# One width for every expert's first tokens, a hinted branch for the rest, and a smaller block for experts of 65 to 128 tokens

## The chip, the cores and the metric

The kernel runs on one core of a Trainium2 chip. The metric is device time in microseconds (us) for one execution. Five engines work side by side and meet through semaphores: TensorE (PE, with its weight loads shown as PEld), VectorE (DVE), ScalarE (ACT), GpSimd (POOL) and SyncE (SP), which here issues most of the transfers. Each engine has its own instruction stream and takes its own branches.

## The reference

One decoder layer on 512 tokens of width 1024: two kinds of token mixing, cross attention, and a mixture of 32 experts, of which every token uses two. Only the last part is touched:

```
g_prob = softmax(xt @ w_group + b_group); best group       # 4 groups of 8 experts
top 2 of softmax(expert logits inside the group)           # 2 experts per token
per expert e: hid = silu(xblk @ w_gate[e]) * (xblk @ w_up[e])
              y   = hid @ w_down[e]                        # 1024 -> 512 -> 1024
out = sum of y * weight over each token's two experts
```

All of it is float32. The 1024 assignments fall unevenly on the experts. With these inputs experts 0 to 31 get 41, 41, 19, 5, 15, 74, 64, 9, 0, 4, 14, 1, 21, 11, 55, 28, 10, 92, 53, 14, 14, 133, 30, 162, 2, 19, 34, 6, 17, 11, 4 and 21 tokens. So 22 experts have at most 32, six have 33 to 64 and four have more than 64: experts 5 (74), 17 (92), 21 (133) and 23 (162). These counts are known only when the program runs.

## The kernel before

The kernel works through the layer in stages; routing ends some 590 us into the profiled execution, and the experts follow. The weights of an expert are 6 MB in six transfers of 1 MB (gate g0, g1, up u0, u1, down d0, d1). SP issues them in expert order (`pump`, the transfer is L815) into a ring of 20 places. A transfer can start when the place's former weights, 20 transfers earlier, have been read for the last time, and it says so by a semaphore of PE.

The loop over experts (L1251 to L1275) is written out 32 times, and the order of instructions on PE, DVE, ACT and POOL is the order in which it is written. For expert `e`:

- `number(e)` (L1211) loads `n` into a register of every engine. Before the loop, `n` was made by counting how many of five limits the expert's number of tokens exceeds (L1044 to L1050): 32, 64, 192, 320 and 448.
- `fetch(rows, later_x[e])` (L1114, on POOL) gathers the tokens behind the first 64 into the one tile `rows` ("xo").
- For odd `e`, `turn_pair` transposes the first 64 tokens of the next two experts on PE (L1122, eight transposes "psgt<-ident,xr").
- A branch on `n > 0` (L1260) chooses `step(now, last, 64)` or `step(now, last, 32)`. A step multiplies the expert's tokens with gate and up (`gate_up`, "psgu"), and in between turns and multiplies down the expert before it (`turn`, "psht<-ident,hs"; `down`, "psy<-wd,hT"). With 64 slots it is 16 matmuls of 512 columns for gate and up, two of them side by side in the array; with 32 slots it is 32 matmuls of 256 columns, four side by side.
- `later_blocks` branches on `n > 1` (L1198). Inside, `block128` computes up to 128 further tokens (transposes "psgt<-ident,xo", then "psg", "psu", "psht<-ident,oh", "psy<-wd,oT"), all in one chain with the result scattered at the end, and a loop (L1202) does further blocks. The loop is not entered with these inputs. An expert's gate and up places in the ring are given back after this branch, since the block may read them.

So every expert's code on PE has two branches of which one or both are jumps: over the width not used, and over the later blocks. The functions that the change touches, and what calls them:

Of the kernel before, what the change touches and what calls it, by code (L numbers as in the profile page):

```python
# [24 lines left out]
KD = D // P  # L25
# [10 lines left out]
FITS = "an expert has at most 512 tokens"  # L36
# [928 lines left out]
def moe(ctx, tc, A, out, x2, x2d, env):  # L965
    nc = tc.nc
    V, SC, PO, PE, SP = nc.vector, nc.scalar, nc.gpsimd, nc.tensor, nc.sync
    bank, ident, before, onesb, f = (env[k] for k in ("bank", "ident", "before", "onesb", "f"))
    tok, mm, pump, W, route, epsr = (env[k] for k in ("tok", "mm", "pump", "W", "route", "epsr"))
# [7 lines left out]
    later_x, later_y = (mc.tile([P, 4, NE], I32, name=f"later_{n}") for n in "xy")  # L977
    ms = ctx.enter_context(tc.tile_pool(name="ms", bufs=1, reuse_waits="tile"))
# [19 lines left out]
    oh, asg = route.oh, route.asg  # L998
# [3 lines left out]
    for i in range(NT):  # L1002
        o = psr[:, i * 32:(i + 1) * 32]
# [8 lines left out]
    d = gp.tile([P, J], F32, name="d")  # L1012
# [29 lines left out]


    steps = iota("steps", [5], [[P, 5]], 0, base=-64)  # L1044
    V.tensor_scalar(steps, steps, 32.0, None, op0=OP.max)
    nb = gp.tile([1, NE, 5], F32, name="nb")
    V.tensor_tensor(nb, cnt[0:1].unsqueeze(2).to_broadcast([1, NE, 5]), steps[0:1].unsqueeze(1).to_broadcast([1, NE, 5]), OP.is_gt)
    nbs = gp.tile([1, NE], F32, name="nbs")
# [48 lines left out]
    def bank(name, tag):  # L1097
        return banks.tile([P, 512], F32, name=name, tag=tag)
# [17 lines left out]

    def turned(xT, rows, copies, tags):

        for a in range(2):
# [2 lines left out]
                PE.transpose(ps[:, k * P:(k + 1) * P], rows[:, a * 512 + k:(a + 1) * 512:4], ident)  # L1122
            copies[a](xT[:, 4 * a:4 * a + 4, :], ps.rearrange("p (k t) -> p k t", t=P))

    class Expert:


        def __init__(self, e):
            self.e, self.c, self.r = e, e // 2, slice(e % 2 * 64, e % 2 * 64 + 64)
            self.x = xT[self.c]  # L1130
            if e % 2 == 0:
                Ys[self.c] = ms.tile([P, D], F32, name="Y", bufs=2)

        def gate_up(self, M, steps):

            e = self.e
            if steps[0] == 0:
                self.ps = bank("psgu", f"g{e % 2}")
            n = P // M // 2
            w = 512 // n  # L1140
            for k in steps:
                for q in range(2 * n):
                    mm(self.ps[q * M:q * M + M, 0:w], self.x[:, k, self.r.start:self.r.start + M],
                       W[e, "ug"[q // n], k // 4][:, k % 4, q % n * w:(q % n + 1) * w], k == 0, k == KD - 1)
            if steps[-1] == KD - 1:
                for q in range(n):
                    h = self.hs[0:M, q * w:(q + 1) * w]
                    SC.activation(h, self.ps[64 + q * M:64 + q * M + M, 0:w], AF.Silu)  # L1148
                    V.tensor_tensor(h, h, self.ps[q * M:q * M + M, 0:w], OP.mult)  # L1149

        def turn(self):
            pt = bank("psht", "h")
            for c in range(4):
                PE.transpose(pt[:, c * 64:(c + 1) * 64], self.hs[:, c // 2 * 256 + c % 2:(c // 2 + 1) * 256:2], ident[0:64, 0:64])  # L1154
            V.tensor_copy(self.hT, pt[:, 0:256])  # L1155

        def down(self):
            e = self.e
            ps = bank("psy", f"y{e % 2}")
            for c in range(4):  # L1160
                for q in range(2):
                    mm(ps[q * 64:q * 64 + 64, :], self.hT[:, c * 64:(c + 1) * 64],
                       W[e, "d", c // 2][:, c % 2, q * 512:q * 512 + 512], c == 0, c == 3)
            for q in range(2):
                SC.copy(Ys[self.c][self.r, q * 512:q * 512 + 512], ps[q * 64:q * 64 + 64, :])  # L1165

        def send(self):
            if self.e % 2:
                scatter(Ys[self.c], first_y[:, self.c:self.c + 1])

    def block128(e, rows, tiles, idx):

        xe, hs, hT = tiles
        tags = "o", f"y{e % 2}"
        turned(xe, rows, (V.tensor_copy, SC.copy), tags)
        ps = {}
        for kind, tag in zip("gu", tags):
            ps[kind] = bank(f"ps{kind}", tag)
            for k in range(KD):
                mm(ps[kind], xe[:, k, :], W[e, kind, k // 4][:, k % 4, :], k == 0, k == KD - 1)  # L1180
            if kind == "g":
                SC.activation(hs, ps["g"], AF.Silu)
        V.tensor_tensor(hs, hs, ps["u"], OP.mult)
# [12 lines left out]
    def later_blocks(e, n, rows):  # L1196

        with tc.If(n > 1):  # L1198
            tiles = [ms.tile([P] + c, F32, name=t) for t, c in (("ox", [KD, P]), ("oh", [512]), ("oT", [512]))]
            block128(e, rows, tiles, later_y[:, 0, e:e + 1])  # L1200
            with tc.If(n > 2):
                with tc.For_i(2, n) as c:  # L1202
                    c = nc.s_assert_within(c - 1, 1, 3, skip_runtime_bounds_check_because=FITS)
                    idx = ms.tile([P, 2], I32, name="oi")
                    for m, t in enumerate((later_x, later_y)):
                        V.tensor_copy(idx[:, m:m + 1], t[:, bass.ds(c, 1), e:e + 1].rearrange("p c e -> p (c e)"))
                    fetch(rows, idx[:, 0:1])
                    block128(e, rows, tiles, idx[:, 1:2])

    def number(e):  # L1210
        return nc.values_load(regs[0:1, e:e + 1], min_val=0, max_val=5, skip_runtime_bounds_check_because=FITS)  # L1211
# [13 lines left out]
    def step(now, last, M):  # L1225

        if M == 64:
            now.gate_up(M, (0, 1))
            last and last.turn()
            now.gate_up(M, (2, 3))  # L1230
            last and last.down()
            now.gate_up(M, (4, 5, 6, 7))
        else:
            now.gate_up(M, (0, 1, 2, 3))
            last and last.turn()
            now.gate_up(M, (4, 5, 6, 7))
            last and last.down()

    with tc.manual_schedule(engines={mybir.EngineType.PE, mybir.EngineType.DVE, mybir.EngineType.Activation, mybir.EngineType.Pool}):
        hs = ms.tile([64, 512], F32, name="hs")  # L1240
        hT = ms.tile([P, 256], F32, name="hT")
        rows = ms.tile([P, D], F32, name="xo")
        fetch_pair(0)
        fetch_pair(1)
        for t in (hs, rows):
            PO.memset(t, 0.0)
        Expert.hs, Expert.hT = hs, hT
        turn_pair(0)
        marks = mark_later_slots()
        last = None  # L1250
        for e in range(NE):  # L1251
            now = Expert(e)
            n = number(e)
            if e > 0:
                fetch(rows, later_x[:, 0, e:e + 1])
            if e % 2 and e < NE - 1:
                turn_pair(e // 2 + 1)
                if e < NE - 3:
                    fetch_pair(e // 2 + 2)
            with tc.If(n > 0) as many:  # L1260
                step(now, last, 64)
            with many.Else():
                step(now, last, 32)
            if last:
                last.send()
                pump(2)
            else:
                later_slots(marks)
                fetch(rows, later_x[:, 0, 0:1])
                cG.close()  # L1270
                env["cT"].close()
# [90 lines left out]
```

## Time and profile before

| | us |
|---|---|
| median of 3 runs (lowest to highest) | 1177.45 (1168.74 to 1178.84) |
| profiled execution, its own time | 1178.46 |
| its span, first to last instruction | 1176.7 |
| PE busy | 991.0 (84%) |
| DVE, ACT, POOL busy | 404.1, 312.6, 279.7 |
| first expert's step to the end of the last one's matmuls | about 590 to 1137 |

In the profile's rows, PE is busy when any matmul runs; a number in square brackets behind a row of the timeline is the time that the engine stood idle ahead of it, with what ended that idle time. "issue" there means that nothing in the profile explains the wait. DMA share is the share of the core's 16 DMA engines that is busy.

### The profile page before, as it was taken

How to read it: one execution, taken by the hardware profiler on the slowest of the kernel's cores; microseconds unless marked ns; L12 is line 12 of the kernel's file. 1: busy time of each engine (PE TensorE's matmuls, PEld its weight loads, DVE VectorE, ACT ScalarE, POOL GpSimd, SP SyncE). 2: the span in 40 equal slices, each digit the busy share in tenths (PEclk: the TensorE clock that was granted, in tenths of full speed). 3: DMA queues.
4: the chain of work that ended last, by engine and by line, in shares of the span. 5: the costliest groups of instructions: out<-in, count | busy, mean ns of one | idle time of the engine just before them, and what ended most of it. 6: DMA issues, size and time to landing. Idle time of an engine off the chain costs nothing. (4 is left out here: it accounts for less than half of the span.)

```text
span 1176.7 us, 16302 instructions
## 1 busy us (share of the span) xinstructions
PE 991.0 (84%) x6260; PEld 649.1 (55%) x6260; DVE 404.1 (34%) x865; ACT 312.6 (27%) x612; POOL 279.7 (24%) x210
## 2 busy tenths in 40 slices
PE   7999999989899999999477997777897887877860
PEld 6787798768688998889223433332332333433320
DVE  8528607656835514345611101111100111011117
ACT  4434423433633534421011101111110101011132
POOL 4431243115124672331211101121101101011112
PEclk9999999999999999999688998898998899998885
DMA  6730231011043452178669959999999949299934
GB/s 206 218 105 24 56 101 37 1 36 55 20 143 93 141 163 71 54 264 332 265 263 413 413 210 397 414 411 414 413 417 400 403 183 407 98 412 412 411 109 180
DMA packets 88618, 269.59 MB, mean 229 GB/s; under 512 B 16191, under 2 KB 57212, under 8 KB 63870
## 3 DMA queue, kind: packets, MB, share of 16 engines
q1 hardware_dynamic: 76926, 252.67, 56.0%
q0 software_dynamic: 10512, 11.04, 2.8%
q10 hardware_dynamic: 1008, 3.67, 0.8%
q8 instruction: 98, 1.61, 0.6%
q14 instruction: 74, 0.61, 0.1%
HBM read 279.91 MB, written 14.68 MB: 250 GB/s over the span
## 5 line engine op out<-in xcount | busy, mean ns | idle before, releaser
L75 PE MATMUL psgu<-wu,xT 128*32 128x256 f32 (+1 forms) x864 | 190.9, 504 | 56.1 <-issue 32.2
L148 POOL TENSOR_TENSOR hl<-raw,hl 128x1024 fp32r<-128x1024 f32 (+1 forms) x67 | 161.4, 2411 | 252.9 <-ACT hl L145 201.9
L75 PE MATMUL psgu<-wg,xT 128*32 128x256 f32 (+1 forms) x864 | 192.8, 504 | 8.7 <-issue 8.7
L75 PEld LDWEIGHTS psgu<-wu,xT 128*32 128x32 f32 (+1 forms) x864 | 66.3, 134 | 151.5 <-issue 119.9
L75 PE MATMUL psy<-wd,hT 128*64 128x512 f32 x512 | 118.4, 600 | 0.7 <-ACTq L1198 0.6
L145 ACT CAST hl<-raw 128x1024 fp32r<-128x1024 f32 (+1 forms) x68 | 70.3, 1040 | 92.0 <-PE psm L75 39.0
L1114 POOL DMA_INDIRECT xo<-x2d,later_x x32 | 32.1, 1004 | 202.8 <-ACTq L1198 55.6
L1155 DVE COPY hT<-psht 128x256 f32<-128x256 f32 x32 | 13.6, 424 | 191.0 <-PE psht L1154 186.2
L1148 ACT ACTIVATE hs<-psgu 32x256 f32<-32x256 f32 (+1 forms) x54 | 22.6, 418 | 208.8 <-PE psgu L75 196.9
L75 PEld LDWEIGHTS psy<-wd,hT 128*64 128x64 f32 x512 | 35.3, 138 | 72.0 <-issue 70.2
L1149 DVE TENSOR_TENSOR hs<-hs,psgu 32x256 f32<-32x256 f32 (+1 forms) x54 | 24.8, 460 | 145.0 <-ACT hs L1148 82.5
L1165 ACT COPY Y<-psy 64x512 f32<-64x512 f32 x64 | 37.1, 580 | 135.2 <-PE psy L75 132.4
L75 PEld LDWEIGHTS psgu<-wg,xT 128*32 128x32 f32 (+1 forms) x864 | 66.8, 134 | 8.7 <-issue 8.4
L75 PE MATMUL psm<-hl,XO 128*128 128x256 f32 x384 | 50.7, 287 | 1.4 <-DVE x L680 1.4
L1122 PE MATMUL psgt<-ident,xr 128*128 128x128 f32 x128 | 22.6, 323 | 33.5 <-PEq L1198 21.2
L75 PE MATMUL psm<-hl,mix 128*128 128x256 f32 x320 | 49.1, 291 | 0.6 <-DVE x L680 0.5
L1106 POOL DMA_INDIRECT yd<-Y,first_y x16 | 16.1, 1009 | 139.4 <-ACTq L1198 125.8
L75 PEld LDWEIGHTS psm<-hl,XO 128*128 128x128 f32 x384 | 47.3, 191 | 2.1 <-DVE x L680 1.8
L75 PE MATMUL psxq<-x1T,hl 128*128 128x512 f32 x192 | 46.7, 396 | 0.0
L75 PEld LDWEIGHTS psm<-hl,mix 128*128 128x128 f32 x320 | 43.5, 193 | 3.5 <-issue 1.3
L75 PE MATMUL psq<-xT,hl 128*128 128x512 f32 x192 | 45.2, 395 | 0.0
L1122 PEld LDWEIGHTS psgt<-ident,xr 128*128 128x128 f32 x128 | 18.5, 212 | 46.2 <-issue 28.9
(368 smaller groups left out, 1669.4 us busy)
## 6 DMA issues: line engine op xcount, KB each, us to landing
wg<-in_moe_w_gate_dram SPq DMA_DIRECT2D x64, 1024.0 KB
wu<-in_moe_w_up_dram SPq DMA_DIRECT2D x64, 1024.0 KB
wd<-in_moe_w_down_dram SPq DMA_DIRECT2D x64, 1024.0 KB
raw<-in_w_in_dram SPq DMA_DIRECT2D x22, 512.0 KB
raw<-in_w_out_dram SPq DMA_DIRECT2D x8, 512.0 KB
raw<-in_xa_wv_dram SPq DMA_DIRECT2D x8, 512.0 KB
raw<-in_xa_wk_dram SPq DMA_DIRECT2D x8, 512.0 KB
raw<-in_xa_wq_dram SPq DMA_DIRECT2D x8, 512.0 KB
```

The source lines that it names most:

```text
L75: PE.matmul(o, l, r, start=start, stop=stop, skip_group_check=True)
L145: cp = SC.copy(hl[:, 0], raw)
L148: (V if n - look < on_dve else PO).tensor_tensor(hl[:, 1], raw, f(hl[:, 0]), OP.subtract)
L1106: t = PO.indirect_dma_start(out=yd, out_offset=bass.IndirectOffsetOnAxis(ap=idx, axis=0), in_=Y, in_offset=None, bounds_check=2 * S - 1, o ...
L1114: PO.indirect_dma_start(out=rows, out_offset=None, in_=x2d, in_offset=bass.IndirectOffsetOnAxis(ap=idx, axis=0), bounds_check=S - 1, oob_i ...
L1122: PE.transpose(ps[:, k * P:(k + 1) * P], rows[:, a * 512 + k:(a + 1) * 512:4], ident)
L1148: SC.activation(h, self.ps[64 + q * M:64 + q * M + M, 0:w], AF.Silu)
L1149: V.tensor_tensor(h, h, self.ps[q * M:q * M + M, 0:w], OP.mult)
L1155: V.tensor_copy(self.hT, pt[:, 0:256])
L1165: SC.copy(Ys[self.c][self.r, q * 512:q * 512 + 512], ps[q * 64:q * 64 + 64, :])
```

## The change

Four things change, all in the experts' part.

1. `step` has one form, with 64 slots, and no branch around it. The first of the five limits becomes 128 in place of 32, so `n` now counts the limits 128, 64, 192, 320 and 448 that are exceeded.
2. `later_blocks` is one branch on `n > 0` with a label. Inside it, `n > 1` (more than 128 tokens) runs `block128` and the loop as before, and otherwise the new `block64` runs.
3. `block64` computes one block of up to 64 tokens with the functions that `Expert` uses for the first 64.
4. In front of each step, PE alone gets a hint that the branch `later{e}` is likely to be taken, that is, that the later code is skipped.

```diff
-    V.tensor_scalar(steps, steps, 32.0, None, op0=OP.max)
+    V.memset(steps[:, 0:1], 128.0)
...
+    def block64(e, rows, tiles, idx):
+
+        xe, hs, hT = tiles[0][:, :, 0:64], tiles[1][0:64], tiles[2][:, 0:256]
+        tags = "o", f"y{e % 2}"
+        for a in range(2):
+            ps = bank("psgt", tags[a])
+            for k in range(4):
+                PE.transpose(ps[:, k * 64:(k + 1) * 64], rows[0:64, a * 512 + k:(a + 1) * 512:4], ident[0:64, 0:64])
+            (SC.copy if a else V.tensor_copy)(xe[:, 4 * a:4 * a + 4, :], ps[:, 0:256].rearrange("p (k t) -> p k t", t=64))
+        ps = bank("psg", "o")
+        gate_up(ps, xe, e, range(KD))
+        hidden(ps, hs)
+        turn(hs, hT)
+        down(bank("psy", tags[1]), hT, e, rows[0:64])
+        scatter(rows, idx)
...
-        with tc.If(n > 1):
-            tiles = [ms.tile([P] + c, F32, name=t) for t, c in (("ox", [KD, P]), ("oh", [512]), ("oT", [512]))]
-            block128(e, rows, tiles, later_y[:, 0, e:e + 1])
-            with tc.If(n > 2):
...
+        with tc.If(n > 0, label=f"later{e}"):
+            with tc.If(n > 1) as more:
+                ts = tiles()
+                block128(e, rows, ts, later_y[:, 0, e:e + 1])
+                with tc.If(n > 2):
...
+            with more.Else():
+                block64(e, rows, tiles(), later_y[:, 0, e:e + 1])
...
-            with tc.If(n > 0) as many:
-                step(now, last, 64)
-            with many.Else():
-                step(now, last, 32)
+            tc.mark_branch_hint_location(f"later{e}", "LikelyTaken", engines=[mybir.EngineType.PE])
+            step(now, last)
```

The functions `gate_up`, `hidden`, `turn` and `down` that `block64` calls are the bodies of the methods of `Expert`, taken out of the class: 16 matmuls of 512 columns, Silu on ACT with a product on DVE, four transposes with a copy, and eight matmuls with two copies on ACT.

On PE, at the end of expert 2's step, where its later code begins. "xo" holds the gathered later tokens, "ox", "oh" and "oT" are the block's tiles. Before:

```order
L1260 UNCONDITIONAL_BRANCH
L1198 COMPARE_AND_BRANCH
L1122 MATMUL psgt<-ident,xo 128x128 x8
L75 MATMUL psg<-wg,ox 128x512 x8
L75 MATMUL psu<-wu,ox 128x512 x8
L1186 MATMUL psht<-ident,oh 128x128 x4
L75 MATMUL psy<-wd,oT 128x512 x8
L1201 COMPARE_AND_BRANCH
```

After the change:

```order
L1221 COMPARE_AND_BRANCH
L1222 COMPARE_AND_BRANCH
L1122 MATMUL psgt<-ident,xo 128x128 x8
L75 MATMUL psg<-wg,ox 128x512 x8
L75 MATMUL psu<-wu,ox 128x512 x8
L1206 MATMUL psht<-ident,oh 128x128 x4
L75 MATMUL psy<-wd,oT 128x512 x8
L1225 COMPARE_AND_BRANCH
```

The jump out of the two widths (L1260) is gone, and the branch to skip (L1221) is followed by the one between the two block sizes (L1222). The block of 128 itself stands as it stood; 36 matmuls lie in it, and 36 more in the loop behind it.

On PE, from the end of expert 2's later code to the first matmul of expert 3, where a skip lands. Before:

```order
L1202 UNCONDITIONAL_BRANCH
L1201 UNCONDITIONAL_BRANCH
L1198 UNCONDITIONAL_BRANCH
L1211 TENSOR_LOAD regs
L1122 MATMUL psgt<-ident,xr 128x128 x8
L1260 COMPARE_AND_BRANCH
L75 MATMUL psgu<-wu,xT 64x512
```

After the change:

```order
L1138 MATMUL psht<-ident,oh 128x64 x4
L75 MATMUL psy<-wd,oT 64x512 x8
L1222 UNCONDITIONAL_BRANCH
L1221 UNCONDITIONAL_BRANCH
L1368 BRANCH_PREFETCH_HINT
L1237 TENSOR_LOAD regs
L1122 MATMUL psgt<-ident,xr 128x128 x8
L75 MATMUL psgu<-wu,xT 64x512
```

The end of the new block of 64 (36 matmuls) now stands last in the skipped code; behind it the hint comes before the register's load, and the step's matmuls follow with no branch between.

## Rows read from the trace of the kernel before

**Rows 1.** The page: span, GB/s in forty slices, the instruction queue.

```profile
span 1176.7 us, 16302 instructions
...
GB/s 206 218 105 24 56 101 37 1 36 55 20 143 93 141 163 71 54 264 332 265 263 413 413 210 397 414 411 414 413 417 400 403 183 407 98 412 412 411 109 180
...
q8 instruction: 98, 1.61, 0.6%
```

**Rows 2.** Stretches: us, engines' busy us (instructions), PE clock, DMA share, GB/s.

```profile
749.00:860.00 111.00, 85.77 (x650) 35.96 (x645) 11.76 (x25) 18.33 (x36) 16.05 (x16) 0.91 1.02 413
...
681.00:695.00 14.00, 11.37 (x27) 4.61 (x25) 2.07 (x3) 0.59 (x1) 0.00 (x0) 0.88 0.04 16
955.00:970.00 15.00, 12.49 (x31) 5.22 (x29) 2.07 (x3) 0.59 (x1) 0.00 (x0) 1.00 0.02 7
1005.00:1025.00 20.00, 18.32 (x45) 7.88 (x43) 1.38 (x2) 1.18 (x2) 0.00 (x0) 1.00 0.01 2
```

**Rows 3.** Waits of SP: us in total, times, longest us.

```profile
SPq L815 <- PEq L1201: 94.7, 4, 33.3
```

**Rows 4.** Timeline of PE, expert 17: step, block of 128, next step.

```profile
848.25 0.64 PE L75 MATMUL psgu<-wu,xT 128*64 128x512 f32 x1
...
859.47 1.23 PE L1122 MATMUL psgt<-ident,xo 128*128 128x128 f32 x8
861.55 7.13 PE L75 MATMUL psg<-wg,ox 128*128 128x512 f32 x16 [0.85 <-DVE ox L1123]
...
877.98 7.10 PE L75 MATMUL psy<-wd,oT 128*128 128x512 f32 x16 [0.83 <-issue]
886.06 0.64 PE L75 MATMUL psgu<-wu,xT 128*64 128x512 f32 x1 [0.98 <-PEq L1201]
```

**Rows 5.** Groups by form, 598 to 1135 us: Silu, product and copy of 64 slots.

```profile
L1148 ACT ACTIVATE hs<-psgu 64x512 f32<-64x512 f32 x9 | 5.3, 594 | 19.4 <-PE psgu L75 19.4
L1149 DVE TENSOR_TENSOR hs<-hs,psgu 64x512 f32<-64x512 f32 x9 | 6.1, 679 | 80.0 <-ACTq L1198 44.4 <-ACT hs L1148 26.7 <-issue 8.9
L1155 DVE COPY hT<-psht 128x256 f32<-128x256 f32 x32 | 13.6, 424 | 191.0 <-PE psht L1154 186.2 <-PE psgu L75 4.8
```

**Rows 6.** Timeline of PE: expert 2's start, and the end of expert 5's block.

```profile
615.26 0.64 PE L75 MATMUL psgu<-wu,xT 128*32 128x256 f32 x2 [5.08 <-PEq L1198]
...
685.24 8.80 PE L75 MATMUL psy<-wd,oT 128*128 128x512 f32 x16 [0.83 <-issue]
```

**Rows 7.** Timeline of PE: ends of blocks 21 and 23, and of expert 31's step.

```profile
962.07 7.11 PE L75 MATMUL psy<-wd,oT 128*128 128x512 f32 x16 [0.83 <-issue]
...
998.34 1.95 PE L1122 MATMUL psgt<-ident,xo 128*128 128x128 f32 x8 [7.06 <-DMA xo<-x2d,later_x]
...
1018.02 7.10 PE L75 MATMUL psy<-wd,oT 128*128 128x512 f32 x16 [0.83 <-issue]
...
1132.70 0.66 PE L1154 MATMUL psht<-ident,hs 64*128 64x64 f32 x4 [0.31 <-PEq L1198]
```

**Rows 8.** Timeline of POOL: the gathers for experts 22 and 23.

```profile
980.63 1.01 POOL L1114 DMA_INDIRECT xo<-x2d,later_x  x1 [8.94 <-DVE xT L1123]
...
989.43 1.01 POOL L1114 DMA_INDIRECT xo<-x2d,later_x  x1 [6.48 <-ACT Y L1165]
```

**Rows 9.** Timeline of PE: first work after expert 24, a 32-slot expert.

```profile
1035.00 1.20 PE L1122 MATMUL psgt<-ident,xr 128*128 128x128 f32 x8 [0.56 <-PEq L1198]
```

**Rows 10.** Timeline of PE: first work after experts 6, 14, 18 and 26, all with 64 slots.

```profile
709.43 1.95 PE L1122 MATMUL psgt<-ident,xr 128*128 128x128 f32 x8 [3.15 <-PEq L1198]
...
817.19 1.20 PE L1122 MATMUL psgt<-ident,xr 128*128 128x128 f32 x8 [2.05 <-DMA xr<-x2d,first_x]
...
899.82 1.42 PE L1122 MATMUL psgt<-ident,xr 128*128 128x128 f32 x8 [2.47 <-PEq L1198]
...
1067.81 1.95 PE L1122 MATMUL psgt<-ident,xr 128*128 128x128 f32 x8 [4.39 <-PEq L1198]
```

**Rows 11.** Timeline of PE: a wait inside a step (expert 3).

```profile
632.44 0.38 PE L75 MATMUL psgu<-wg,xT 128*32 128x256 f32 x1 [2.65 <-issue]
```

More of the change, by code (lines that the diff above doesn't have):

```diff
@@ L1123, in turned, with gate_up, hidden, turn @@
             copies[a](xT[:, 4 * a:4 * a + 4, :], ps.rearrange("p (k t) -> p k t", t=P))
+    def gate_up(ps, x, e, steps):
+        for k in steps:
+            for q in range(2):
+                mm(ps[q * 64:q * 64 + 64, :], x[:, k, :], W[e, "ug"[q], k // 4][:, k % 4, :], k == 0, k == KD - 1)
+    def hidden(ps, hs):
+        SC.activation(hs, ps[64:128, :], AF.Silu)
+        V.tensor_tensor(hs, hs, ps[0:64, :], OP.mult)
+    def turn(hs, hT):
+        pt = bank("psht", "h")
+        for c in range(4):
+            PE.transpose(pt[:, c * 64:(c + 1) * 64], hs[:, c // 2 * 256 + c % 2:(c // 2 + 1) * 256:2], ident[0:64, 0:64])
+        V.tensor_copy(hT, pt[:, 0:256])
+    def down(ps, hT, e, Y):
+        for c in range(4):
+            for q in range(2):
+                mm(ps[q * 64:q * 64 + 64, :], hT[:, c * 64:(c + 1) * 64],
+                   W[e, "d", c // 2][:, c % 2, q * 512:q * 512 + 512], c == 0, c == 3)
+        for q in range(2):
+            SC.copy(Y[:, q * 512:q * 512 + 512], ps[q * 64:q * 64 + 64, :])
     class Expert:
@@ L1129, in __init__, with gate_up @@
             self.e, self.c, self.r = e, e // 2, slice(e % 2 * 64, e % 2 * 64 + 64)
-            self.x = xT[self.c]
+            self.x = xT[self.c][:, :, self.r]
             if e % 2 == 0:
                 Ys[self.c] = ms.tile([P, D], F32, name="Y", bufs=2)
-        def gate_up(self, M, steps):
-            e = self.e
+        def gate_up(self, steps):
             if steps[0] == 0:
[L1138 to L1144, printed above, removed]
+                self.ps = bank("psgu", f"g{self.e % 2}")
+            gate_up(self.ps, self.x, self.e, steps)
             if steps[-1] == KD - 1:
[L1146 to L1149, printed above, removed]
+                hidden(self.ps, hs)
         def turn(self):
[L1152 to L1155, printed above, removed]
+            turn(hs, hT)
         def down(self):
[L1158 to L1165, printed above, removed]
+            down(bank("psy", f"y{self.e % 2}"), hT, self.e, Ys[self.c][self.r])
         def send(self):
@@ L1196, in later_blocks, with tiles @@
     def later_blocks(e, n, rows):
-        with tc.If(n > 1):
-            tiles = [ms.tile([P] + c, F32, name=t) for t, c in (("ox", [KD, P]), ("oh", [512]), ("oT", [512]))]
-            block128(e, rows, tiles, later_y[:, 0, e:e + 1])
-            with tc.If(n > 2):
[L1202 to L1208, printed above, removed]
+        def tiles():
+            return [ms.tile([P] + c, F32, name=t) for t, c in (("ox", [KD, P]), ("oh", [512]), ("oT", [512]))]
+        with tc.If(n > 0, label=f"later{e}"):
[3 more added lines that the diff above has]
+                with tc.If(n > 2):
+                    with tc.For_i(2, n) as c:
+                        c = nc.s_assert_within(c - 1, 1, 3, skip_runtime_bounds_check_because=FITS)
+                        idx = ms.tile([P, 2], I32, name="oi")
+                        for m, t in enumerate((later_x, later_y)):
+                            V.tensor_copy(idx[:, m:m + 1], t[:, bass.ds(c, 1), e:e + 1].rearrange("p c e -> p (c e)"))
+                        fetch(rows, idx[:, 0:1])
+                        block128(e, rows, ts, idx[:, 1:2])
+            with more.Else():
+                block64(e, rows, tiles(), later_y[:, 0, e:e + 1])
     def number(e):
@@ L1223, in turn_pair, with step @@
         turned(xT[c], xr[c], (V.tensor_copy, SC.copy), ("t0", "t1"))
[L1225 to L1237, printed above, removed]
+    def step(now, last):
+        now.gate_up((0, 1))
+        last and last.turn()
+        now.gate_up((2, 3))
+        last and last.down()
+        now.gate_up((4, 5, 6, 7))
     with tc.manual_schedule(engines={mybir.EngineType.PE, mybir.EngineType.DVE, mybir.EngineType.Activation, mybir.EngineType.Pool}):
@@ L1246, in moe @@
             PO.memset(t, 0.0)
-        Expert.hs, Expert.hT = hs, hT
         turn_pair(0)
```

1 line of the change is left out of this document (added).

## The prediction

> **What bounds the kernel now.** I read the page first, then stretches of it, then SP's waits, then PE's timeline. Behind the routing the experts are a stream of weights: the page's GB/s stand at 400 and over in most slices from about 600 us on, up to 1118, with holes at three places [rows 1]. From 749 to 860 us the transfers are saturated (413 GB/s, DMA share 1.02) while PE works 85.8 of 111 us [rows 2]: there PE is not the bound. In the holes it is the other way round: from 681 to 695, 955 to 970 and 1005 to 1025 us the DMA share is 0.04 and less while PE is nearly always busy [rows 2]. SP's longest waits, four with 94.7 us in all, are for PE's sequencer at L1201, the end of the later code [rows 3]: the ring is full, and the next places come free only when the block of 128 of expert 5, 21 or 23 is over. Expert 17's block makes no hole by itself, but puts PE so far behind that expert 21's does. So 49 us of the stream stand still because PE is late, and towards the end PE is late again: expert 31's gate, up and the down of expert 30 end at 1132.70 - 0.31 = 1132.4 [rows 7], after the last slice with a full stream has ended [rows 1]. What counts is PE's path on two pieces, from the end of expert 1 to the block of expert 5, and from expert 17's block to the end.
>
> **The change part by part.** A step with 64 slots takes 859.47 - 848.25 = 11.2 us [rows 4]. I price the new path with it for every expert, and compare whole pieces, so that the 32-slot steps need no price of their own; the dearer steps are in the sum.
>
> *Block of 64, for experts 5 and 17.* The block of 128 takes 861.55 - 859.47 for its transposes and copies and then to 877.98 + 7.10 = 885.08, so 25.6 us in all [rows 4]. A block of 64 has the matmuls of a step (11.2, all of it TensorE's own work), as many transposes as before (at most 1.2), and waits that a step hides: copies of x (at most 0.85 [rows 4]), Silu 0.59, product 0.68, copy 0.42 [rows 5], and some 0.4 of handing over between them, my choice. Sum 15.3. Bounds: 12.4 with no wait at all, 25.6 if it were no better than the old one. I take 15.3, since every wait in it has a row.
>
> *The wait g from an expert's last matmul to the next one's first.* It is the one disputed price, since the change moves what lies there. Its floor is 0.56 us after a 32-slot expert, seen eight times (0.55 to 0.61) [rows 9]. After the four 64-slot experts that have no block and are followed by transposes it is 3.15, 2.05, 2.47 and 4.39, mean 3.0 [rows 10] (one of them is put down to a gather). By the order of PE's instructions a skip after 32 slots passes 72 matmuls, one after 64 slots the 44 of the unused width as well, 116, and a skip in the change 36 + 36 + 36 = 108. So without a hint the nearest rows are those of [rows 10], g = 3.0; with a hint that does what it says, g = 0.56 is the nearest. To it come waits inside steps (2.65 in the row shown [rows 11]; eight of them in 31 experts, 0.9 to 2.7, 13.5 in all), 0.44 per expert, which I keep: g = 1.0. Bounds 0.56 and 4.39.
>
> These waits look like instruction loading: the instruction queue moved 98 packets with 1.61 MB, 16 KB each [rows 1], and "issue" means that nothing else explains them. [...]
>
> *Piece 1, end of expert 1 to the end of expert 5's block.* Before: 615.26 - 5.08 = 610.2 to 685.24 + 8.80 = 694.0, 83.8 us [rows 6]. After: four steps 44.8, two pairs of transposes 2.4 [rows 9], block 15.3, four waits: 62.5 + 4g. The stream would stand still from 681 on, 70.8 us after the start, so with g under 2.1 the first hole is gone: 14 us.
>
> *Between.* Experts 6 to 17 are then paced by the stream as before, 14 us earlier, if PE keeps up. PE needs to the end of expert 17's step 610.2 + 62.5 + 4g + 1.0 + 12 steps 134.4 + six pairs of transposes 7.2 + 11g = 815.3 + 15g; the stream allows 859.5 - 14 = 845.5. So PE hides behind the stream up to g = 2.0. For scale, 6.29 MB at 413 GB/s are 15.2 us an expert [rows 2] against 11.2 + 0.6 + g on PE.
>
> *Piece 2, expert 17's block to the end of expert 31's step.* Before: 859.47 to 1132.4, 272.9 us. After: block 15.3, joint 1.0, experts 18 to 21 44.8 + 2.4 + 3g, block of 128 of expert 21 25.6. Then 29.2 from its end, 962.07 + 7.11, to the next block's start at 998.34 [rows 7], which I leave as it is: PE waits 7.06 there for a gather, because the gathers for experts 22 and 23 start one after the other, at 980.63 and 989.43 [rows 8], behind expert 21's scatter; two steps that are 3 us dearer use up that wait. Then block 23, 998.34 to 1025.12, 26.8 [rows 7], joint 1.3, experts 24 to 31 89.6 + 3.6 + 7g. Sum 239.6 + 10g, with g = 1.0 249.6, so 23.3 us less. Expert 21's block would end at 859.5 + 92.1 = 951.6, before the stream stands still at 955: the second hole goes too. The third stays, at some 20 us. With the first two holes gone the stream ends some 29 us earlier, at about 1092, and PE by its own sum at 1095, so PE's sum counts.
>
> *Nothing else.* One memset for one tensor_scalar, the branch's compare and the hint are one instruction each; on ACT and DVE one wide Silu and product (1.27 us [rows 5]) stand for two narrow ones, under PE's next matmuls. Were that cover gone, 1.3 us per expert would show. [...]
>
> Sum: 1178.46 of the profiled execution - 14 - 23.3 = **1141 us**. The median of the runs is 1 us lower than the profiled one; I leave that out.
>
> **The rivals.** With g over 2.0, both pieces and what lies between are PE's own: the end of expert 31's step is at 815.3 + 15g + 239.6 + 10g = 1054.9 + 25g, against 1132.4 before. Break-even is g = 3.1.
>
> *The hint does nothing* (it names a branch that the sequencer then fetches as always). g = 3.0: 1130 at that point, 2 us less than before, **1176 us**. For it: the four rows of [rows 10] and no row that shows a hint working. Against: the hint stands some 11 us ahead of its branch, and the longest wait is 4.4. Chance 0.16. A hint that helps half the time, g = 2.0, gives 1104.9, 27 less, 1151: chance 0.10.
>
> [...] Chance 0.16.
>
> **How the numbers follow.** Forecast 0.58. With the lowest g and the lowest block the sum is 1178.5 - 14 - (23.3 + 2.9 + 4.4), 1134; I go to 1128 for what PE's clock may give. Above, the range takes in the half hint and the first rival with its spread: 1182. Left out are most of the slower rival and a little below, under 0.2. The forecast's own range is 1128 to 1152. A difference under 1%, 12 us, counts as none. Faster by over 1% means g under 2.6: 0.58 + 0.10 = 0.68. Within 1%: 0.16. Slower: 0.16.
>
> **What would show it.** The hole after expert 5 and the one at expert 21 gone, the one at expert 23 still there; blocks of 64 of about 15 us; waits on PE between experts near 0.6 us and seldom over 2; experts 24 to 31 in about 100 us. Wrong if waits of 2 to 4 us stand behind every skip, if the gathers of experts 22 and 23 take longer than 29 us, or if PE waits for weights in the last eight experts.

## The result, and the profile after

The change makes the kernel faster. The median is 1137.86 us in four runs (1137.5 to 1139.3), against 1175.47 us for the kernel before in four runs beside it (1168.74 to 1178.84). The ratio is 0.967, with a 95% interval of 0.964 to 0.971. The profiled execution took 1137.84 us.

The page of the changed kernel: the engines' busy time, share and instructions, TensorE's granted clock (PEclk, in tenths of full speed) and GB/s in forty slices, the instruction queue with packets and MB, and one of PE's two largest groups of matmuls (32 experts, eight matmuls each, two MATMULs for one in the trace).

```profile
span 1136.0 us, 14628 instructions
...
PE 1014.6 (89%) x5556; PEld 638.9 (56%) x5556; DVE 398.8 (35%) x841; ACT 310.0 (27%) x592; POOL 279.4 (25%) x210
...
PEclk9999999999999999999959999998899999999985
...
GB/s 214 203 131 19 38 94 75 2 19 19 57 111 112 91 170 130 56 98 319 280 233 318 414 415 415 413 415 414 415 417 415 412 409 414 121 407 413 415 187 192
...
q8 instruction: 91, 1.49, 0.5%
...
L75 PE MATMUL psgu<-wu,xT 128*64 128x512 f32 x512 | 245.2, 613 | 21.7 <-DMA wu<-in_moe_w_up_dram 14.7
```

Of the three holes in GB/s [rows 1], one is left (121). PE is busy for 23.6 us longer than before although the span is 40.7 us shorter: the wide steps cost more, and most of the waits are gone. The same stretches as in [rows 2], and the one hole that is left:

```profile
681.00:695.00 14.00, 13.34 (x68) 5.58 (x68) 2.02 (x4) 2.34 (x4) 2.91 (x3) 1.00 1.01 416
749.00:860.00 111.00, 93.66 (x420) 33.14 (x418) 10.81 (x19) 14.99 (x26) 12.02 (x12) 0.94 1.02 415
955.00:970.00 15.00, 11.13 (x40) 4.81 (x37) 1.37 (x2) 2.34 (x4) 2.01 (x2) 0.80 1.02 417
974.00:993.00 19.00, 16.48 (x41) 7.01 (x39) 2.07 (x3) 1.18 (x2) 0.00 (x0) 1.00 0.06 23
```

From 681 to 695 us 416 GB/s stand where 16 stood, and from 955 to 970 us 417 where 7 stood. The hole from 974 to 993 us lies under the block of expert 23. SP's waits (us in total, times, longest) for the end of the block of 128 say the same. L1225 is what was L1201 [rows 3]:

```profile
SPq L815 <- PEq L1225: 36.6, 2, 30.1
```

PE's timeline answers to [rows 4, 6, 7, 9, 10]. The stretches are the starts of experts 2 and 3, the block of 64 of expert 5, that of expert 17, the start and the end of expert 21's block of 128 and the step behind it, expert 23's block, and expert 31:

```profile
613.12 0.61 PE L75 MATMUL psgu<-wu,xT 128*64 128x512 f32 x1 [0.66 <-DMA wu<-in_moe_w_up_dram]
...
625.15 1.23 PE L1122 MATMUL psgt<-ident,xr 128*128 128x128 f32 x8 [0.73 <-DMA xr<-x2d,first_x]
...
662.63 1.17 PE L1182 MATMUL psgt<-ident,xo 64*128 64x64 f32 x8
664.44 0.64 PE L75 MATMUL psg<-wu,ox 128*64 128x512 f32 x1 [0.64 <-DVE ox L1183]
...
672.93 0.69 PE L1138 MATMUL psht<-ident,oh 64*128 64x64 f32 x4 [1.41 <-DVE oh L1133]
674.14 5.19 PE L75 MATMUL psy<-wd,oT 128*64 128x512 f32 x16 [0.52 <-DVE oT L1139]
679.16 0.59 PE L75 MATMUL psgu<-wu,xT 128*64 128x512 f32 x1
...
844.98 1.17 PE L1182 MATMUL psgt<-ident,xo 64*128 64x64 f32 x8
...
856.49 3.65 PE L75 MATMUL psy<-wd,oT 128*64 128x512 f32 x16 [0.52 <-DVE oT L1139]
...
909.75 1.23 PE L1122 MATMUL psgt<-ident,xo 128*128 128x128 f32 x8
...
929.61 5.74 PE L75 MATMUL psy<-wd,oT 128*128 128x512 f32 x13
...
936.37 0.61 PE L75 MATMUL psgu<-wu,xT 128*64 128x512 f32 x1 [1.01 <-DMA wu<-in_moe_w_up_dram]
...
964.60 1.98 PE L1122 MATMUL psgt<-ident,xo 128*128 128x128 f32 x8 [3.87 <-DMA xo<-x2d,later_x]
...
993.17 0.61 PE L75 MATMUL psgu<-wu,xT 128*64 128x512 f32 x1 [1.01 <-PEq L1225]
...
1093.06 0.66 PE L1138 MATMUL psht<-ident,hs 64*128 64x64 f32 x4 [1.55 <-DVEq L1221]
```

Expert 2 starts 0.66 us after expert 1, where it waited 5.08 [rows 6]. The block of 64 takes 674.14 + 5.19 - 662.63 = 16.7 us for expert 5 and 856.49 + 3.65 - 844.98 = 15.2 us for expert 17. The first figure holds 5.19 us for matmuls that take 3.65 in the second: the granted clock was 0.70 in that stretch and 1.00 in the second. Behind a block of 64 the next step follows without a gap (679.16), where a block of 128 is followed by 1.01 us. Expert 31's step ends at 1093.06 - 1.55 = 1091.5. From there to the end of the span are 44.5 us, and 44.3 before: the tail is untouched.

### The profile page after: what moved, and what is told of

Same layout as the page of the kernel before. It is cut to its first block, busy times and chain, and to the rows that moved or that the text cites. A ratio compares the mean times of both kernels' runs of the same rounds, so it can differ in the third digit from the quotient of the medians.

```text
span 1136.0 us, 14628 instructions
## 1 busy us (share of the span) xinstructions
PE 1014.6 (89%) x5556; PEld 638.9 (56%) x5556; DVE 398.8 (35%) x841; ACT 310.0 (27%) x592; POOL 279.4 (25%) x210
## 5 line engine op out<-in xcount | busy, mean ns | idle before, releaser
L75 PE MATMUL psgu<-wu,xT 128*64 128x512 f32 x512 | 245.2, 613 | 21.7 <-DMA wu<-in_moe_w_up_dram 14.7
L75 PE MATMUL psgu<-wg,xT 128*64 128x512 f32 x512 | 245.4, 614 | 0.0
L75 PEld LDWEIGHTS psgu<-wu,xT 128*64 128x64 f32 x512 | 66.4, 139 | 151.5 <-issue 124.9
L1133 DVE TENSOR_TENSOR hs<-hs,psgu 64x512 f32<-64x512 f32 x32 | 21.7, 679 | 286.6 <-ACTq L1221 250.8
L1147 ACT COPY Y<-psy 64x512 f32<-64x512 f32 x64 | 37.1, 579 | 264.9 <-PE psy L75 264.5
L75 PEld LDWEIGHTS psy<-wd,hT 128*64 128x64 f32 x512 | 37.1, 139 | 74.2 <-issue 72.4
L75 PEld LDWEIGHTS psgu<-wg,xT 128*64 128x64 f32 x512 | 66.5, 139 | 1.3 <-issue 1.3
L414 DVE TENSOR_REDUCE st<-pss 128x1 f32<-128x128 f32 (+1 forms) x64 | 30.6, 487 | 35.9 <-PE pss L75 34.7
L75 PEld LDWEIGHTS psq<-xT,hl 128*128 128x128 f32 x192 | 36.0, 188 | 8.9 <-issue 0.2
L75 PEld LDWEIGHTS psxq<-x1T,hl 128*128 128x128 f32 x192 | 35.6, 188 | 8.1
L415 ACT ACTIVATE Pt<-pss,st 128x128 f32<-128x128 f32 (+1 forms) x64 | 33.6, 530 | 20.1 <-DVE st L414 17.8
```

The lines of the kernel that those rows point to most:

```text
L75: PE.matmul(o, l, r, start=start, stop=stop, skip_group_check=True)
L414: V.tensor_reduce(st[:, 0, i:i + 1], ps[:, 0:n], AX.X, OP.max, negate=True)
L415: SC.activation(Pt[:, offp[i]:offp[i] + n], ps[:, 0:n], AF.Exp, bias=st[:, 0, i:i + 1], accum_out=st[:, 1, i:i + 1])
L1133: V.tensor_tensor(hs, hs, ps[0:64, :], OP.mult)
L1147: SC.copy(Y[:, q * 512:q * 512 + 512], ps[q * 64:q * 64 + 64, :])
```

## The experiments

The theory is that of the forecast: the hint has the target of the skip loaded ahead (a supposition), and the block of 64 frees the weights' places earlier. The rival is that the single width makes the gain and the hint does nothing. All times are medians. Ratios are against the kernel before, run beside each, with 95% intervals. Beside the changed kernel the kernel before took 1175.5 us, beside the other groups of runs 1177.9 to 1181.0, so a difference of a few us between two groups is judged by the ratios.

### The parts taken apart

**The change without its hint.**

```diff
-            tc.mark_branch_hint_location(f"later{e}", "LikelyTaken", engines=[mybir.EngineType.PE])
```

> The change with the hint taken out and nothing else moved. Theory A (the hint brings PE the code behind the skip in time): the waits between experts return to 2 to 3 us on average, near those seen before behind 64-slot experts, and the time goes to 1155 to 1178 us. Theory B (the waits went because the branch between two widths went; the hint does nothing): the waits stay near 0.66 us and the time stays at 1138 us, within 3 us.

Measured: 1165.2 us, ratio 0.985 (0.983 to 0.988), 27 us more than with it (ratio 0.967). PE's waits from 600 to 1150 us (us in total, times, longest):

```profile
PE psgu L75 <- issue: 26.4, 22, 1.9
PE psgt L1122 <- PEq L1221: 8.3, 14, 0.7
```

PE's timeline of that run where an expert begins:

```profile
1053.53 1.20 PE L1122 MATMUL psgt<-ident,xr 128*128 128x128 f32 x8 [0.57 <-PEq L1221]
1054.66 1.07 PE L75 MATMUL psgu<-wu,xT 128*64 128x512 f32 x2
1056.78 0.59 PE L75 MATMUL psgu<-wg,xT 128*64 128x512 f32 x1 [1.04 <-issue]
```

The skip itself lands after 0.57 us. The wait stands some 2 us later, inside the step, where nothing in the profile explains it. It costs more than its 1.04 us, since the matmuls of "wu" ahead of it ran alone (1.07 for two) and not beside those of "wg". Experts 24 to 31 take 112.2 us in place of 98.3. So the hint works, and what it takes away is this wait: in the changed kernel it stands once, with 0.6 us.

**The hint alone, on the kernel before.** It names the branch over the later blocks and stands ahead of the branch over the width.

```diff
+            tc.mark_branch_hint_location(f"later{e}", "LikelyTaken", engines=[mybir.EngineType.PE])
             with tc.If(n > 0) as many:
...
-        with tc.If(n > 1):
+        with tc.If(n > 1, label=f"later{e}"):
```

> The kernel before with the hint alone, put ahead of the branch between the two widths and naming the branch over the later blocks. Theory A: the waits behind skips fall to about 0.6 us, those behind the jump over the 64-slot code stay at 2 to 4 us in most 32-slot experts, and the holes of the weight stream stay in part: 1150 to 1170 us. Theory B, or a hint that is lost when another branch is executed in between: as before, 1175 us.

Measured: 1169.1 us, ratio 0.990 (0.986 to 0.994). PE's waits in the kernel before, from 590 to 1135 us:

```profile
PE psgu L75 <- issue: 40.9, 15, 4.6
PE psgt L1122 <- PEq L1198: 21.2, 14, 4.4
PE psgu L75 <- PEq L1198: 12.5, 4, 5.1
```

The same waits with the hint, from 600 to 1150 us:

```profile
PE psgu L75 <- issue: 40.0, 17, 4.0
...
PE psgt L1122 <- PEq L1198: 16.4, 14, 2.5
...
PE psgu L75 <- PEq L1198: 8.1, 5, 2.3
```

Counted from 600 us in both, the waits behind the named branch (L1198) fall from 33.0 to 24.5 us, and not to 0.6 us each as theory A had it: eight of the 19 stay at 1.5 to 2.5 us. Those inside the steps stay at 40 us: the jump over the width that is not used has no hint. With two jumps in each expert, a hint for one of them is worth 1%.

**The change with blocks of 128 for all four experts.** The first limit is 64, so that experts 5 and 17 run the block of 128.

```diff
-    V.memset(steps[:, 0:1], 128.0)
+    V.memset(steps[:, 0:1], 64.0)
```

> The change with the first limit 64 in place of 128, so that experts 5 and 17 run the block of 128; hint and single width stay, and the code is the same. Theory A: expert 5's block ends 9 us later and makes a hole of some 5 us in the weight stream, expert 17's adds 10 us to PE's path behind it: 1150 to 1157 us. Rival: with short waits PE catches up before expert 21, the block of 64 is hidden, and the time stays within 3 us of 1138.

Measured: 1156.3 us, ratio 0.979 (0.976 to 0.982), as theory A had it: the block of 64 is not hidden.

**One width alone**, with neither hint nor block of 64 (both edits above).

> One width alone: no hint, and the block of 128 for experts 5 and 17. Theory A: waits of 2 to 3 us on a path of PE that is 20 us longer than that of the change: 1170 to 1195 us, no better than before. Theory B: the branch between two widths was the cost, so it equals the run with the hint and without the block of 64.

Measured: 1193.4 us, ratio 1.012 (1.008 to 1.016): slower than before. SP's waits for the end of a block of 128, with the hint and blocks of 128:

```profile
SPq L815 <- PEq L1225: 83.7, 4, 34.5
```

The same without the hint:

```profile
SPq L815 <- PEq L1225: 107.0, 4, 32.4
```

With four blocks of 128 the ring is full four times, as before (94.7, four times [rows 3]), and twice in the changed kernel (36.6). In medians the hint is worth 1193.4 - 1156.3 = 37.1 us with blocks of 128 and 1165.2 - 1137.9 = 27.3 with blocks of 64. The block of 64 is worth 28.2 without the hint and 18.4 with it, so the two overlap by about 10 us. The 27.3 and the 18.4 are taken across two groups of runs; by the ratios they are some 21 and 14 us, and the overlap is some 17. One width by itself costs 1.2%. The rival is out: the wider steps pay only once the waits behind the jumps are gone.

### Is it the jump, or what it passes?

**A short skip without hint.** The later code is one block of 128.

```diff
-            with tc.If(n > 1) as more:
...
-            with more.Else():
-                block64(e, rows, tiles(), later_y[:, 0, e:e + 1])
+            block128(e, rows, tiles(), later_y[:, 0, e:e + 1])
...
-            tc.mark_branch_hint_location(f"later{e}", "LikelyTaken", engines=[mybir.EngineType.PE])
```

> No hint, and the later code holds one block of 128 alone (no loop, no block of 64): a skip passes 36 matmuls in place of 108. What it leaves out, the blocks behind 192 tokens, is not entered with these inputs; experts 5, 17, 21 and 23 run a block of 128, as in the variant without hint and without the block of 64 (1193.4 us), which it is compared with. Theory (the wait inside each step is loading of code that was skipped to, so it depends on how much code is passed): the waits inside steps, 0.5 to 2.2 us there and in nearly every expert, become fewer or shorter, and the time falls by 10 to 35 us, to 1158 to 1183 us; its lower end is the hinted variant with the block of 128 (1156.3). Rival (a taken branch that is not announced costs the same whatever it passes): the waits stay at 1 to 1.9 us in each step, and the time stays within 6 us of 1193.

Measured: 1141.1 us, ratio 0.970 (0.964 to 0.976), 52 us under the same work with 108 matmuls to skip. That is beyond the expected range, and without the hint or the block of 64 nearly as fast as the changed kernel. The jump by itself is not what costs.

**The same with the hint.**

```diff
+            tc.mark_branch_hint_location(f"later{e}", "LikelyTaken", engines=[mybir.EngineType.PE])
             step(now, last)
```

> The short later code (one block of 128 alone, 36 matmuls to skip; blocks behind 192 tokens left out, not entered with these inputs) with the hint put back ahead of each step. Compared with the same without hint (1141.1 us). Theory (the hint is worth only the loading that it hides, and a short skip hides none: its trace has no wait inside the steps): the time is the same within 6 us, 1137 to 1148, if anything 1 to 3 us dearer, since a hinted skip took 0.65 us and this one 0.56. Rival (the hint removes a cost of every taken branch, whatever it passes): 10 us or more faster, under 1131.

Measured: 1145.3 us, ratio 0.972 (0.969 to 0.975), the same. But this run doesn't test what it was meant to. Its trace shows all 32 hints executed between 0.8 and 3.7 us, at the start of the program and not ahead of the steps; in the changed kernel 31 of them stand ahead of their steps. Why they moved is not shown. It repeats the run above, and whether a hint in place would gain anything on a short skip was not measured.

**72 matmuls to skip, without hint**: the block of 128 and the block of 64, no loop.

```diff
-                with tc.If(n > 2):
-                    with tc.For_i(2, n) as c:
...
-                        block128(e, rows, ts, idx[:, 1:2])
...
-            tc.mark_branch_hint_location(f"later{e}", "LikelyTaken", engines=[mybir.EngineType.PE])
```

> The changed kernel without the hint and without the loop behind the block of 128: a skip passes 72 matmuls (block of 128 and block of 64) in place of 108; the blocks behind 192 tokens are left out, not entered with these inputs. Theory (the wait grows with the code that is passed: none at 36 matmuls, about 1.4 us an expert at 108): waits of 0.3 to 1 us inside many steps, 1140 to 1155 us, between the hinted kernel (1137.9) and the one without hint (1165.2). Rival (a threshold: what passes more than about 36 matmuls always has to be loaded): as many and as long waits as at 108, 1160 us and more.

Measured: 1133.2 us, ratio 0.961 (0.958 to 0.965), likely a little faster than the changed kernel, though the two intervals still touch (0.964 to 0.971 there). Both expectations were wrong: there are no waits inside the steps at all, so the cost does not grow evenly with the code passed.

**108 matmuls, without hint and without loop**: one more block of 128, written straight, in the loop's place.

```diff
-                    with tc.For_i(2, n) as c:
...
+                    fetch(rows, later_x[:, 1, e:e + 1])
+                    block128(e, rows, ts, later_y[:, 1, e:e + 1])
```

> Without the hint, as the variant that took 1165.2 us, but the loop behind the block of 128 is replaced by one more block of 128 written straight: a skip passes 108 matmuls as there, with no loop in it (no jump back, no hint of the loop's own, no index registers). Blocks behind 320 tokens are left out, not entered with these inputs. Theory (what makes the waits is the amount of code passed): waits of 0.8 to 1.9 us inside nearly every step as there, 1160 to 1170 us. Rival (what makes them is the loop: its jump back or the hint that stands in it takes the place of the skip's target): no such waits, 1130 to 1140 us, as with 72 matmuls to skip (1133.2).

Measured: 1153.9 us, ratio 0.981 (0.976 to 0.986), between the two expectations. The waits are back, in another place: right behind the skip, 2.1 to 2.7 us at 15 of 26 skips, and 0.56 to 0.65 at the others.

**180 matmuls**: the loop written out as three more blocks of 128, each under its own branch (`more_blocks`), in the hinted kernel with two tiles (below).

```diff
-                    with tc.For_i(2, n) as c:
...
+                more_blocks(e, n, rows, ts, 1)
```

> For any number of tokens and without a loop: the hinted kernel with two tiles for the gathered tokens (1134.1 us), the loop behind the block of 128 written out as three more blocks of 128, each under its own branch. A skip passes 180 matmuls in place of 108. Theory (the hint has the skip's target loaded ahead, however much code is passed): waits between experts stay at 0.65 to 0.85 us, none inside the steps, 1131 to 1137 us. Rival (the hint hides only skips of about the length of before, or the larger program takes the chip longer to load): waits of 1 to 2.5 us behind the skips return, 1150 us or more.

Measured: 1189.6 us, ratio 1.010 (1.008 to 1.013). Again there is no loop, and the trace shows all 32 hints executed by 3.7 us: it is a run without hint at 180 matmuls, and says nothing on how far a hint in place would reach. Waits of over 2 us stand behind nearly every skip. PE's waits for its sequencer ahead of a pair's transposes, from 600 to 1150 us, with 36 matmuls passed and no hint:

```profile
PE psgt L1122 <- PEq L1221: 7.7, 13, 0.7
```

With 72:

```profile
PE psgt L1122 <- PEq L1221: 8.2, 13, 0.9
```

With 108, all straight:

```profile
PE psgt L1122 <- PEq L1221: 19.9, 13, 2.7
```

With 180:

```profile
PE psgt L1122 <- PEq L1229: 29.0, 13, 2.4
```

Thirteen waits each: 0.59, 0.63, 1.53 and 2.23 us on average. PE's path through experts 24 to 31, from the first gate or up matmul of 24 to the last of 31 in each timeline, with the same number of matmuls in each:

| matmuls passed by a skip | hint in place | experts 24 to 31, us | median, us |
|---|---|---|---|
| 36 | no | 98.0 | 1141.1 (blocks of 128 only) |
| 72 | no | 98.1 | 1133.2 |
| 108, straight | no | 109.4 | 1153.9 |
| 108, a third of them in a loop | no | 112.2 | 1165.2 |
| 108, a third of them in a loop | yes | 98.3 | 1137.9 |
| 180 | no | 117.1 | 1189.6 (two tiles) |

So the cost comes with the length of what is skipped: nothing up to 72 matmuls, 11 us in eight experts at 108, 14 with a third of them in a loop, 19 at 180. A hint in place, measured with the loop alone, takes nearly all of it back. Not all of the cost is waiting. The mean granted clock over these experts was 1.00 at 36, at 72 and with the hint in place, but 0.97 at 108 straight, 0.98 with the loop and 0.96 at 180. In the kernel before, the clock was 0.50 from 998.34 to 1001.74 us, behind the wait of 7.06 us [rows 7], and 0.51 from 1067.81 to 1071.21, behind that of 4.39 [rows 10]. That the lower means come from such stretches behind the waits is an estimate.

The branch itself gives a reason why nothing is seen up to 72. These are PE's own branches at the line of the later code (count, with four ends of blocks in the first row, then the shortest, the middle and the longest in ns, then the first and last start in us) with 36, 72, 108 straight and 180 matmuls passed, and with 108 in part in a loop, first without and then with the hint:

```profile
L1221 PEldq COMPARE_BRANCH  x36: 70/218/358, 593.4 to 1087.9; - x36
...
L1221 PEldq COMPARE_BRANCH  x32: 65/338/2694, 592.7 to 1076.6; - x32
...
L1221 PEldq COMPARE_BRANCH  x32: 70/3018/6452, 597.5 to 1098.7; - x32
...
L1229 PEldq COMPARE_BRANCH  x32: 82/6060/6898, 592.7 to 1135.5; - x32
...
L1221 PEldq COMPARE_BRANCH  x32: 70/2272/3128, 597.4 to 1120.4; - x32
...
L1221 PEldq COMPARE_BRANCH  x32: 78/2426/3538, 597.3 to 1087.1; - x32
```

At 36 no branch takes more than 0.36 us. At 72 eight take 2.2 to 2.7 us; at 108 straight ten take 2.3 to 3.2 and fourteen 6.0 to 6.5; at 180 twenty-five take 5.9 us or more. PE's sequencer is ahead of its matmuls: the last branch of the changed kernel starts at 1087.1 us, and the matmuls ahead of it end at 1091.5. So 4.4 us of work were still queued when that skip began. With the same lead at every skip, an estimate from this one, a branch of 2.4 us is hidden whole, and one of 6.1 leaves 1.7 us on top of the 0.56. Fourteen of the fifteen long waits at 108 stand behind the fourteen long branches. The hint does not shorten the branch: the middle one takes 2.4 us with it and 2.3 without. What it takes away is the later wait, inside the step. That it does so by having code loaded ahead, as the theory says, was supposed and is not shown; the instruction queue moved 91 packets with the hint and 91 without.

In the trace a block of 36 matmuls is 60 MATMULs (its twelve transposes are one each, the others two) and as many LDWEIGHTS: 60 of each from 964.60 to 992.2 us, expert 23's block in the changed kernel. By an estimate from that count 36, 72, 108 and 180 matmuls are some 120, 240, 360 and 600 instructions. Branches of over 2 us then begin between 120 and 240: none at 120, eight at 240, and 24 of the 28 taken ones at 360. What no run settles is why, with the loop in the skipped code, the wait shows 2 us behind the landing and not at it, and how the hint takes it away.

### Better versions

**Two tiles for the later tokens**, used in turn by even and odd experts.

```diff
-        rows = ms.tile([P, D], F32, name="xo")
+        later_rows = [ms.tile([P, D], F32, name=f"xo{k}") for k in range(2)]
...
             n = number(e)
+            rows = later_rows[e % 2]
```

> The changed kernel with two tiles for the gathered later tokens, used in turn by even and odd experts (the table of the limits' comparisons becomes BF16 to make room). The gather for expert 23 then need not wait until expert 22's has been overwritten or expert 21's scatter has read its rows. Theory (PE's 3.87 us wait ahead of expert 23's block is the gathers' series on one tile, and from there to the end PE is the bound): the wait is gone, the block of expert 23 starts some 4 us earlier, the half-clock stretch behind the wait (964 to 971 us) goes with it, worth up to 3.4 us, and the time falls by 4 to 7 us, to 1131 to 1134 us. Rival (the hole in the weight stream behind expert 23 or POOL's own work sets the end): the wait shrinks but the end stays within 1.5 us of 1137.9.

Measured: 1134.1 us, ratio 0.964 (0.960 to 0.969); profiled executions 1134.4 and 1137.8. The intervals of this kernel and the changed one overlap, so 3.7 us less is likely but not settled by the times. The traces are clear. In the changed kernel POOL issues the gather for expert 23 nine microseconds behind that for expert 22. POOL's timeline there:

```profile
946.45 1.00 POOL L1114 DMA_INDIRECT xo<-x2d,later_x  x1 [8.59 <-DMA yd<-xo,later_y]
...
955.43 1.01 POOL L1114 DMA_INDIRECT xo<-x2d,later_x  x1 [6.66 <-DMA xo<-x2d,later_x]
```

After the wait for it PE's granted clock is 0.51, as this stretch of the changed kernel shows, with the columns as above:

```profile
964.00:971.00 7.00, 6.40 (x14) 3.55 (x15) 0.69 (x1) 0.58 (x1) 0.00 (x0) 0.51 0.98 406
```

With two tiles expert 23's block starts with no wait for a gather, and the clock there is 1.00:

```profile
959.88 1.23 PE L1122 MATMUL psgt<-ident,xo 128*128 128x128 f32 x8
...
961.00:968.00 7.00, 6.15 (x15) 2.77 (x15) 0.91 (x2) 0.58 (x1) 0.00 (x0) 1.00 1.01 421
```

**Two tiles and 72 matmuls to skip, without hint.**

> The two best edits together: no hint and no loop (a skip passes the block of 128 and the block of 64, 72 matmuls; blocks behind 192 tokens left out, not entered with these inputs), and two tiles for the gathered tokens, used in turn. Theory (PE's path from expert 23 to the end sets the time, so the 3.15 us wait for the gather ahead of its block, and the half clock behind it, come off): 1126 to 1131 us, 3 to 6 under the same with one tile (1133.2). Rival (the weight stream now ends last, since PE waits for weights at two of the last eight experts there): within 1.5 us of 1133.2.

Measured: 1129.1 us, ratio 0.959 (0.955 to 0.963), the lowest median of all. Its interval is clear of the changed kernel's, but not of those of the two edits alone. It serves experts with up to 192 tokens only.

**A loop over blocks of 128 as the whole later code.**

```diff
+            with tc.For_i(1, n) as c:
+                c0 = nc.s_assert_within(c - 1, 0, 3, skip_runtime_bounds_check_because=FITS)
...
+                block128(e, rows, tiles(), idx[:, 1:2])
+                fetch(rows, idx[:, 0:1])
```

> A version for any number of tokens with short later code: no hint and no block of 64; one block of 128 is the body of the loop over the later blocks, which gathers the next block's tokens at its end, so a skip passes 36 matmuls; two tiles for the gathered tokens, used in turn. Theory (short code needs no hint, and the gathers' wait at expert 23 is gone): no waits inside the steps, 0.56 us between experts, no wait for a gather ahead of expert 23's block: as the short code without hint (1141.1) less the 3.9 us of that wait, plus about 1 us of loop for each of the four blocks, 1135 to 1143 us. Rival (entering and closing the loop makes PE wait 3 to 5 us per block for code): 1150 us or more.

Measured: 1193.6 us, ratio 1.013 (1.009 to 1.016), so the rival's wait is there, at two to three times its price. Its reason, code to load, is not what the trace points to. PE's waits behind the loop, from 600 to 1150 us:

```profile
PE psgu L75 <- PEq L1232: 38.6, 4, 10.6
```

POOL's timeline where the loop ends behind expert 5:

```profile
686.75 1.01 POOL L1107 DMA_INDIRECT yd<-xo,oi  x1 [38.55 <-DVE xo L1214]
690.06 1.02 POOL L1115 DMA_INDIRECT xo<-x2d,oi  x1 [2.30 <-DMA yd<-xo,oi]
694.65 0.99 POOL L1115 DMA_INDIRECT xo<-x2d,later_x  x1 [3.57 <-PEq L1232]
```

PE has done its part at 685.2 and goes on at 694.2, four microseconds after the loop's gather was issued: 9.7 us for each of the four blocks, where the expectation's 1 us and its rival's 3 to 5 were guesses that no run had shown. In all four PE goes on 1.8 to 2.0 us after the loop's gather has landed. That it waits for the scatter and the gather in the loop to land is read from this order, not tested by itself. Of the versions for any number of tokens, the hinted kernel with two tiles has the lowest median.

## Why the prediction was right

It said 1141 us and the profiled execution took 1137.8. By its steps:

- **The wait g**, taken as 1.0, was 0.65 to 0.78 us at the skips, but for two that end in a wait for weights. Over experts 24 to 31, 98.3 us less 89.6 for steps and 3.6 for transposes leave 5.1 for seven waits, 0.73 each. The floor of 0.56 became 0.65, and the 0.44 for waits inside steps fell to almost nothing: they went with the hint too, which the forecast had not said. The reading behind the floor was kind: the trace before has it seven times, not eight, and behind three more 32-slot experts PE waited 1.57, 1.88 and 3.06 us. The forecast took the best rows for the hinted case without a row that showed a hint, and the runs without it show that the hint did make the difference. How it does so they leave open.
- **The block of 64** was 16.7 and 15.2 us against 15.3. The waits in it were 0.64, 1.41 and 0.52 us, for the copy, for Silu with the product, and for hT. What the first has more is its last matmuls at a clock of 0.70.
- **Piece 1** was forecast at 66.5 us with g = 1.0. It took from 613.12 - 0.66 = 612.5 to 679.3, 66.9. So close a match is partly luck: the block is 1.4 us longer, and the rest, with its shorter waits, 1.0 us shorter. The first hole is gone. It began 2.3 us later than before, which the forecast left out. Expert 17's block starts at 844.98, against a forecast of 845.5: between, the stream sets the pace, and ahead of experts 14 and 16 PE waits 4.0 and 6.1 us for weights.
- **Piece 2** took from 844.98 to 1091.5, 246.5 us against 249.6. Ten waits that are 0.27 us shorter make 2.7 of the 3.1. The joint behind the block of 64, forecast at 1.0, is nothing, and expert 23's block took 27.6 us in place of 26.8: its start ran at a clock of 0.51, where the kernel before had 0.64. The second hole is gone, the third stays at some 20 us, and the 29.2 us of the gathers' chain stand to the tenth: from 929.61 + 5.74 = 935.35, the end of expert 21's block, to 964.60.
- **The clock** has no term in the sum, but it is in the prices: the step of 11.2 us and the block of 25.6 come from stretches at 1.00, so the sum took 1.00 nearly throughout. That came true. The 6 us by which the range goes below the lowest sum, for the clock, are a guess that no run shows. Over piece 1 the mean granted clock was 0.97 and over piece 2 0.99, where the kernel before had 0.90 and 0.91; 0.51 stands for some 7 us behind the wait for the gather. So a part of the gain is likely clock that the kernel before lost behind its waits; no run separates the two.
- **The rivals.** *The hint does nothing* is out. Its g was near what the kernel without the hint has: by experts 24 to 31, (112.2 - 93.2) / 7 = 2.7 against 3.0. Its time was less near: the median without the hint is 1165.2 us, 16 below the kernel before beside it, where that rival had 2 (the profiled execution, 1172.5, was the slowest of five). The place was not right either: the rows showed waits at the skip, and without the hint they stand inside the step. The slower outcome, at 0.16, did not come: no skip of the changed kernel has a wait of over 0.8 us for PE's sequencer. One width alone is slower than before, at 1193.4 us, with four blocks of 128 and no hint.

What the forecast missed is a shorter way to the same end: it priced g by whether there is a hint, and counted the 108 matmuls that a skip passes, but did not ask what g would be at 72.

## What to carry to other kernels

Code that is rarely run and stands in line with the rest can cost each time it is skipped, by its length (here from somewhere between 72 and 108 matmuls on, 11 us in eight experts at 108 and 19 at 180). Shorten it before anything else, then announce the jump, and look at the order of the instructions for where the hint really stands. Price each step on the stretch whose bound it shifts: here PE's longer steps were free wherever the stream was late (PE waited 4.0 and 6.1 us for weights ahead of experts 14 and 16), and each microsecond of block or wait counted from expert 17 on.

## What the runs showed of the hardware

- From the last matmul ahead of a skip to the first behind it PE stood 0.56 us at the least at 108 straight, and 0.65 with a hint executed there in the changed kernel, so by an estimate from the two a hint in place costs about 0.1 us.
- PE's sequencer reached the last branch of the changed kernel 4.4 us ahead of the end of its matmuls. Behind that kernel's branches, 2.4 us in the middle, PE stood 0.65 to 0.78 us; behind those of 6.0 to 6.5 us at 108 straight it stood 2.1 to 2.7.
- The wait that comes with a longer skip need not stand where the jump lands: with the loop in the skipped code, without hint, the landing took 0.57 us, and 1.04 us came some 2 us into the step, put down to "issue" (22 waits put down so at the steps' gate and up, 26.4 us in all).
- Closing a loop with a scatter and a gather in it held PE for 8.9 to 10.6 us, four times.
